# A mean over rows of 8192 floats on one core: the rows in three zones of 3, 108 and 17 per partition instead of two of 111 and 17, with another first and last load and three stores

## The chip, the core and the metric

The kernel runs on one core of a Trainium2 chip. That core has a TensorE (not used here), VectorE (DVE), ScalarE (ACT), GpSimd (POOL) and SyncE (SP), and sixteen DMA engines that move data between the memory in which the input lies and the on-chip buffers of 128 partitions. SP issues all DMAs of this kernel. The metric is the device time of one execution in microseconds, lower is better; shown are the median of several runs and one execution under the hardware profiler.

## The reference

```python
x = np.random.randn(64, 256, 8192).astype(np.float32)
def reference(x):
    return np.mean(x, axis=2)
```

The input is 16384 rows (64 x 256) of 8192 floats, 32 KiB each, 512 MiB in all. Each row becomes one number, its mean; the output has 64 KiB.

## The kernel before

**Zones.** The 16384 rows are dealt to 128 partitions, 128 rows to each. They are dealt in zones: a zone of n rows per partition covers 128 x n adjacent rows of the input, and partition p takes n adjacent rows of it, so neighbouring partitions read n x 32 KiB apart. There are two zones, of 111 and 17 rows (`ZONE`, `FROM`; `EARLY` and `LATE` are their sizes). Rows are counted per partition from 0 to 127; `rows_of(n, k)` names rows n to n + k - 1 of all partitions, which must lie in one zone.

**Buffers.** `two` holds two rows per partition (8 MiB in all), `four` holds four (16 MiB). Each is single: it is loaded anew when those who read it are done. `two_free` and `four_free` count who is done, `two_sem` and `four_sem` count landed loads (16 for each DMA). `res` takes the sum of each row, in the order of the rows; `scaled` takes the first zone's means, `ends` the second's, `fin` the last piece of the last row and its partial sums. `turn` takes three sums of a round before they are copied to `res`.

**Who sums.** DVE sums both rows of `two` with one reduction (`pair`, L169), and rows 0 to 2 of `four` with a helper, `halves` (L151), that adds the two halves of a row and sums the result in one instruction (`quad` calls it row by row). ScalarE sums the fourth row of `four` with an activation that accumulates (`row`, L218). After the loop, in `REST`, DVE takes two rows of `four` and ScalarE two. GpSimd multiplies the sums by 1/8192 (L91 for the first zone, L97 for the second).

**Order.** The order is written out by hand on SP's queue:

1. rows 111 and 110 into `two` in three DMAs of 1, 3 and 4 MiB (L109 to L111; `first_sem`), then rows 0 to 3 into `four` (L112, `second_sem`);
2. a loop of 17 rounds of six rows: wait until `two` is free, load two rows (L115, L116), wait until `four` is free, load four (L117, L118);
3. `REST`: loads of 2, 4, 2, 4 and 2 rows (112, 106, 114, 116, 120), waiting likewise (L124, L127);
4. rows 122 and 123 into the front half of `four` (`HALF`, L129), rows 124 and 125 into `two` (`LASTP`, L131);
5. the last two rows, 126 and 127, in five pieces at `cuts` (L136). The first holds row 126 and the first quarter of row 127. The later ones have 3840, 1280, 576 and 448 columns, the last of them into `fin`, the others into the back half of `four`;
6. when GpSimd has scaled the first zone and the fourth piece has landed, the store of `scaled` (L141); when `late_sem` says that `ends` is complete, the store of `ends` (L143); then the wait for both (L144).

DVE and ScalarE split each piece of the last row between them (`mine` gives ScalarE's columns); the partial sums go beside the last piece in `fin`, so that one last `halves` over 456 columns, already scaled, gives the mean of row 127 (L151, output `ends`). It waits for the last piece and for `NPART` partial sums on `last_sem`.

Of the kernel before, what the change touches and what calls it, by code (L numbers as in the profile page):

```python
# [6 lines left out]
ADD = mybir.AluOpType.add  # L7
X = mybir.AxisListType.X
# [3 lines left out]
def bass_global_avg_pool_1d_kernel(  # L12
# [4 lines left out]
    P = 128  # L17
    ALIGN = 4096
    B, C, L = x.shape
    rows = B * C  # L20
# [3 lines left out]


    OWN = rows // P
    ZONE = [111, 17]
    FROM = [0, ZONE[0]]
    EARLY, LATE = ZONE
    ROUNDS = (ZONE[0] - 9) // 6  # L30
    REST = [(112, 2), (106, 4), (114, 2), (116, 4), (120, 2)]
    HALF, LASTP = 122, 124
    assert rows % P == 0 and sum(ZONE) == OWN and 8 + 6 * ROUNDS == ZONE[0] - 1
    FIRST = L // 4


    U = L // 256
    cuts = [0, L + 64 * U, L + 184 * U, L + 224 * U, L + 242 * U, 2 * L]
    mine = [64 * U, 43 * U, 13 * U, 4 * U]
    LAST = cuts[5] - cuts[4]  # L40
    NPART = 8

    flat = x.rearrange("b c l -> (b c) l")
    out_flat = out.rearrange("b c -> (b c)")
# [4 lines left out]
    out_zone = [  # L49
        out_flat[P * f : P * (f + n)].rearrange("(p r) -> p r", p=P)  # L50
        for f, n in zip(FROM, ZONE)
    ]

    with ExitStack() as ctx:
        sb = lambda n, s: ctx.enter_context(nc.sbuf_tensor(n, s, F32))
        sem = lambda n: ctx.enter_context(nc.semaphore(n))
        res = sb("res", [P, OWN - 1])
        scaled = sb("scaled", [P, EARLY])
        ends = sb("ends", [P, LATE])
        fin = sb("fin", [P, LAST + NPART])  # L60
# [12 lines left out]
        first_sem = sem("first_sem")  # L73
        second_sem = sem("second_sem")
        chunk_sems = [sem(f"chunk_sem{c}") for c in range(4)]
# [6 lines left out]
        tail = four[:, 2 * L : 4 * L]  # L82
        part = lambda n: fin[:, LAST + n : LAST + n + 1]

        eng = nc.gpsimd
        eng.sem_inc(turn_sem, 2)
        eng.memset(part(NPART - 1), 0.0).then_inc(last_sem, 1)  # L89
        eng.wait_ge(four_free, 4)  # L90
        eng.tensor_scalar(  # L91
            scaled[:], res[:, 0:EARLY], inv, None, op0=mybir.AluOpType.mult
        ).then_inc(pool_sem, 1)
        eng.wait_ge(two_free, 5)
        eng.wait_ge(four_free, 6)
        eng.wait_ge(owned_sem, 4)
        eng.tensor_scalar(  # L97
            ends[:, 0 : LATE - 1], res[:, EARLY : OWN - 1], inv, None,
            op0=mybir.AluOpType.mult,
# [2 lines left out]

        eng = nc.sync
        def rows_of(n, k):
            z = 1 if n >= FROM[1] else 0
            return zone[z][:, (n - FROM[z]) * L : (n - FROM[z] + k) * L]

        a, z = rows_of(ZONE[0] - 1, 1), rows_of(ZONE[0], 1)
        eng.dma_start(two[:, L : L + FIRST], z[:, 0:FIRST]).then_inc(first_sem, 16)  # L109
        eng.dma_start(two[:, L + FIRST : 2 * L], z[:, FIRST:L]).then_inc(first_sem, 16)  # L110
        eng.dma_start(two[:, 0:L], a).then_inc(first_sem, 16)  # L111
        eng.dma_start(four[:], rows_of(0, 4)).then_inc(second_sem, 16)  # L112
        src = rows_of(4, 6 * ROUNDS).rearrange("p (i w) -> p i w", i=ROUNDS)
        with eng.Fori(0, ROUNDS) as i:
            eng.wait_ge(two_free, 1).then_inc(two_free, -1)  # L115
            eng.dma_start(two[:], src[:, bass.ds(i, 1), 0 : 2 * L]).then_inc(two_sem, 16)  # L116
# [12 lines left out]
        eng.dma_start(four[:, 0 : 2 * L], rows_of(HALF, 2)).then_inc(four_sem, 16)  # L129
        eng.wait_ge(two_free, 5)  # L130
        eng.dma_start(two[:], rows_of(LASTP, 2)).then_inc(two_sem, 16)  # L131
        last = rows_of(OWN - 2, 2)
        for c in range(5):
            a, z = cuts[c], cuts[c + 1]
            dst = tail[:, a:z] if c < 4 else fin[:, 0:LAST]
            eng.dma_start(dst, last[:, a:z]).then_inc(  # L136
                chunk_sems[c] if c < 4 else last_sem, 16
            )
        eng.wait_ge(pool_sem, 1)
        eng.wait_ge(chunk_sems[3], 16)  # L140
        eng.dma_start(out_zone[0], scaled[:]).then_inc(out_sem, 16)  # L141
        eng.wait_ge(late_sem, 2)
        eng.dma_start(out_zone[1], ends[:]).then_inc(out_sem, 16)  # L143
        eng.wait_ge(out_sem, 32)  # L144


        eng = nc.vector

        def halves(ap, to, done=None, scale=1.0):
            n = ap.shape[1] // 2  # L150
            made = eng.tensor_tensor_reduce(  # L151
                ap[:, 0:n],
                ap[:, 0:n],
                ap[:, n : 2 * n],
                scale=scale,
                scalar=0.0,
                op0=ADD,
                op1=ADD,
                accum_out=to,
            )  # L160
            if done is not None:
                made.then_inc(done, 1)

        rows_in = lambda ap: ap.rearrange("p (j l) -> p j l", l=L)
        at = lambda n, k: res[:, n : n + k]
        sums = res[:, 4 : 4 + 6 * ROUNDS].rearrange("p (i w) -> p i w", i=ROUNDS)

        def pair(to, ap=two[:]):
            eng.tensor_reduce(to, rows_in(ap), X, ADD).then_inc(two_free, 1)  # L169

        def quad(to, done=four_free):
            for j, ap in enumerate(to):
                halves(
                    four[:, j * L : (j + 1) * L], ap, done if j == len(to) - 1 else None
                )

        eng.wait_ge(first_sem, 48)
        pair(at(ZONE[0] - 1, 2))
        eng.wait_ge(second_sem, 16)
        quad([at(j, 1) for j in range(3)])  # L180
        with eng.Fori(0, ROUNDS) as i:
            now = sums[:, bass.ds(i, 1), :]
            eng.wait_ge(two_sem, 16).then_inc(two_sem, -16)  # L183
# [3 lines left out]
            quad([turn[:, j : j + 1] for j in range(3)], turn_sem)  # L187
            eng.wait_ge(turn_sem, 1).then_inc(four_free, 1)
            eng.tensor_copy(  # L189
                now[:, :, 2:5], turn[:].rearrange("p (i w) -> p i w", i=1)  # L190
            ).then_inc(turn_sem, 1)
        for k, (n, size) in enumerate(REST):
            eng.wait_ge(two_sem if size == 2 else four_sem, 16 * (k // 2 + 1))
            if size == 4:
                quad([at(n, 1), at(n + 1, 1)])
            elif k < len(REST) - 1:
                pair(at(n, 2))
            else:
                pair(at(n, 1), two[:, 0:L])
        eng.wait_ge(four_sem, 48)  # L200
        eng.tensor_reduce(  # L201
            at(HALF, 2), rows_in(four[:, 0 : 2 * L]), X, ADD
        ).then_inc(owned_sem, 1)
        eng.wait_ge(two_sem, 64)
        eng.tensor_reduce(at(LASTP, 1), two[:, 0:L], X, ADD).then_inc(owned_sem, 1)  # L205
        eng.wait_ge(chunk_sems[0], 16)
        halves(tail[:, 0:L], res[:, OWN - 2 : OWN - 1], owned_sem)
        for c in range(1, 4):
            eng.wait_ge(chunk_sems[c], 16)
            halves(tail[:, cuts[c] + mine[c] : cuts[c + 1]], part(3 + c), last_sem)  # L210
        eng.wait_ge(last_sem, 16 + NPART)
        halves(fin, ends[:, LATE - 1 : LATE], late_sem, inv)

# [1 line left out]
        eng = nc.scalar  # L215

        def row(ap, to):
            return eng.activation(ap, ap, COPY, accum_out=to)  # L218

        fourth, second = four[:, 3 * L : 4 * L], two[:, L : 2 * L]  # L220
        eng.wait_ge(second_sem, 16)
        row(fourth, at(3, 1)).then_inc(four_free, 1)
        with eng.Fori(0, ROUNDS) as i:
            eng.wait_ge(four_sem, 16).then_inc(four_sem, -16)  # L224
            eng.sem_inc(go_sem, 1)
            row(fourth, sums[:, bass.ds(i, 1), 5:6]).then_inc(four_free, 1)
        for k, (n, size) in enumerate(REST):
            if size == 4:
                eng.wait_ge(four_sem, 16 * (k // 2 + 1))
                row(four[:, 2 * L : 3 * L], at(n + 2, 1))  # L230
                row(fourth, at(n + 3, 1)).then_inc(four_free, 1)
        eng.wait_ge(two_sem, 48)
        row(second, at(REST[-1][0] + 1, 1)).then_inc(two_free, 1)
        eng.wait_ge(two_sem, 64)
        row(second, at(LASTP + 1, 1)).then_inc(owned_sem, 1)
        for c in range(4):
            eng.wait_ge(chunk_sems[c], 16)
            a = cuts[c] if c else L
            ap = tail[:, a : a + mine[c]]
            eng.activation(ap, ap, COPY, accum_out=part(c)).then_inc(last_sem, 1)  # L240


# [26 lines left out]
```

## Time and profile before

| | |
|---|---|
| median of three runs | 1242.95 us (1242.9 to 1242.98) |
| the profiled execution, its own time | 1243.15 us |
| its span, first to last instruction | 1241.8 us |
| moved by DMA | 536.94 MB, 432 GB/s over the span |
| busy: DVE, ACT, POOL | 643.0, 176.5, 2.3 us |

The profile is that of one execution. In its rows from the timeline the first number is the start in us from the beginning of the span, the second the duration in us; then come engine, line of the kernel, operation, output and input with their shapes (partitions x elements), and in brackets how long the engine had been idle and what ended that. "SPq" rows are DMA issues on SP: their duration is that of issuing, not of the transfer. A wait in the loop shows as "ACTq" or "DVEq", the engine's own sequencer; the data that it waited for came by DMA. In the row of the queue stand packets, megabytes and the share of the sixteen engines' span that the packets took. In the table of DMA issues, the last number is the time from issue to landing.

### The profile page before, as it was taken

The page shows a single profiled execution, that of the slowest core. Times are in us where ns is not written, and L with a number is a line of the kernel's source. Part 1 is how long each engine was busy: PE and PEld are TensorE (multiplying, and loading weights), DVE is VectorE, ACT ScalarE, POOL GpSimd, SP SyncE. Part 2 cuts the span into 40 slices and gives each one's busy share as a digit, 9 for nine tenths or more (in the row PEclk, how much of TensorE's full clock was granted, in tenths as well). Part 3 has the DMA queues.
Part 4 walks back from the last instruction along what each step waited for, and adds up shares of the span by engine and source line. Part 5 has one row for each costly group of instructions (what it writes and reads, how often), then busy time and mean ns, then how long its engine had stood idle before and what let it go on. Part 6 is the DMA issues. An engine that isn't in the chain of part 4 may idle for free. (4 is left out here: it accounts for less than half of the span.)

```text
span 1241.8 us, 713 instructions
## 1 busy us (share of the span) xinstructions
DVE 643.0 (52%) x166; ACT 176.5 (14%) x57; POOL 2.3 (0%) x7
## 2 busy tenths in 40 slices
DVE  2373836454544637383736454554638383625257
ACT  0021020202020202012020202020202102040423
POOL 0000000000000000000000000000000000000000
DMA  9999999999999999999999999999999999999998
GB/s 405 439 439 439 439 431 414 439 439 439 439 439 422 422 439 439 439 439 439 422 422 439 439 439 439 439 422 422 439 439 439 439 439 424 420 439 439 439 439 374
DMA packets 10048, 536.94 MB, mean 432 GB/s; under 512 B 1088, under 2 KB 1216, under 8 KB 1472
## 3 DMA queue, kind: packets, MB, share of 16 engines
q1 hardware_dynamic: 10048, 536.94, 99.8%
HBM read 536.87 MB, written 0.07 MB: 432 GB/s over the span
## 5 line engine op out<-in xcount | busy, mean ns | idle before, releaser
L151 DVE CUSTOM_DVE_ANT_0 four<-four 128x4096 f32<-128x4096 f32 (+3 forms) x62 | 260.5, 4248 | 434.7 <-DVEq L186 366.7
L169 DVE TENSOR_REDUCE res<-two 128x16384 f32 (+2 forms) x21 | 353.1, 16814 | 145.4 <-DVEq L183 96.3
L218 ACT ACTIVATE four<-four 128x8192 f32<-128x8192 f32 x22 | 154.6, 7029 | 1017.9 <-ACTq L224 864.3
L201 DVE TENSOR_REDUCE res<-four 128x2 f32<-128x16384 f32 x1 | 17.2, 17220 | 10.6 <-DMA four<-in_x_dram 10.6
L218 ACT ACTIVATE two<-two 128x8192 f32<-128x8192 f32 x2 | 14.1, 7030 | 36.7 <-DMA two<-in_x_dram 36.7
L205 DVE TENSOR_REDUCE res<-two 128x1 f32<-128x8192 f32 x1 | 8.7, 8686 | 2.1 <-DMA two<-in_x_dram 2.1
L240 ACT ACTIVATE four<-four 128x2048 f32<-128x2048 f32 (+3 forms) x4 | 4.1, 1030 | 7.7 <-DMA four<-in_x_dram 7.5
L189 DVE COPY res<-turn 128x3 f32 x17 | 2.9, 170 | 4.2 <-DVE turn L151 4.2
L151 DVE DVE_READ_ACCUMULATOR2_ANT turn<- 128x1 f32 x51 | 4.2, 83 | 0.0
L218 ACT ACTIVATION_READ_ACCUMULATOR four<-four (+1 forms) x22 | 4.1, 187 | 0.0
L91 POOL TENSOR_SCALAR scaled<-res 128x111 f32<-128x111 f32 x1 | 0.5, 503 | 1117.6 <-ACT four L218 1117.6
L97 POOL TENSOR_SCALAR ends<-res 128x16 f32<-128x16 f32 x1 | 1.5, 1499 | 117.9 <-DVE res L151 117.9
L218 ACT ACT_TABLE_LOAD x1 | 1.3, 1283 | 0.7 <-PEq L254 0.7
L240 ACT ACTIVATION_READ_ACCUMULATOR four<-four 128x1 f32 x4 | 0.7, 186 | 0.0
L151 DVE DVE_READ_ACCUMULATOR2_ANT res<- 128x1 f32 x8 | 0.7, 82 | 0.0
L151 DVE CUSTOM_DVE_ANT_0 fin<-fin 128x228 f32<-128x228 f32 x1 | 0.4, 397 | 0.2 <-ACT four L240 0.2
L218 ACT ACTIVATION_READ_ACCUMULATOR two<-two 128x1 f32 x2 | 0.4, 186 | 0.0
L151 DVE DVE_READ_ACCUMULATOR2_ANT fin<- 128x1 f32 x3 | 0.2, 82 | 0.0
L254 POOL MEMSET const-bfloat16-1.0<- 128x1 bf16 x1 | 0.1, 101 | 0.0
L254 POOL MEMSET const-uint8-127<- 128x1 uint8 x1 | 0.1, 101 | 0.0
L254 POOL MEMSET const-float32-0.0<- 128x1 f32 x1 | 0.1, 99 | 0.2 <-issue 0.2
L89 POOL MEMSET fin<- 128x1 f32 x1 | 0.1, 98 | 0.4 <-POOLq L254 0.4
(2 smaller groups left out, 0.2 us busy)
## 6 DMA issues: line engine op xcount, KB each, us to landing
four<-in_x_dram SPq DMA_DIRECT2D x1, 5120.0 KB, 41.6
two<-in_x_dram SPq DMA_DIRECT2D x1, 4096.0 KB, 20.9
two<-in_x_dram SPq DMA_DIRECT2D x1, 3072.0 KB, 11.7
four<-in_x_dram SPq DMA_DIRECT2D x1, 1920.0 KB, 45.7
two<-in_x_dram SPq DMA_DIRECT2D x1, 1024.0 KB, 4.9
four<-in_x_dram SPq DMA_DIRECT2D x1, 640.0 KB, 46.8
four<-in_x_dram SPq DMA_DIRECT2D x21, 44.1
two<-in_x_dram SPq DMA_DIRECT2D x21, 40.2
```

What stands on the lines that cost most here:

```text
L89: eng.memset(part(NPART - 1), 0.0).then_inc(last_sem, 1)
L91: eng.tensor_scalar(scaled[:], res[:, 0:EARLY], inv, None, op0=mybir.AluOpType.mult).then_inc(pool_sem, 1)
L97: eng.tensor_scalar(ends[:, 0 : LATE - 1], res[:, EARLY : OWN - 1], inv, None, op0=mybir.AluOpType.mult,).then_inc(late_sem, 1)
L151: made = eng.tensor_tensor_reduce(ap[:, 0:n], ap[:, 0:n], ap[:, n : 2 * n], scale=scale, scalar=0.0, op0=ADD, op1=ADD, accum_out=to,)
L169: eng.tensor_reduce(to, rows_in(ap), X, ADD).then_inc(two_free, 1)
L189: eng.tensor_copy(now[:, :, 2:5], turn[:].rearrange("p (i w) -> p i w", i=1)).then_inc(turn_sem, 1)
L201: eng.tensor_reduce(at(HALF, 2), rows_in(four[:, 0 : 2 * L]), X, ADD).then_inc(owned_sem, 1)
L205: eng.tensor_reduce(at(LASTP, 1), two[:, 0:L], X, ADD).then_inc(owned_sem, 1)
L218: return eng.activation(ap, ap, COPY, accum_out=to)
L240: eng.activation(ap, ap, COPY, accum_out=part(c)).then_inc(last_sem, 1)
L254: nc = _bacc.Bacc("TRN2", target_bir_lowering=False, num_devices=1)
```

## The change

The zones become 3, 108 and 17 rows per partition. The three rows of the first zone are loaded first, in pieces of 1, 3 and 8 MiB, into the first three rows of `four`; DVE sums rows 0 and 1 with `halves`, ScalarE row 2. Nothing is loaded into `two` ahead of the loop; GpSimd increments `two_free` once at its start, so that the loop's first load of `two` can be issued. The loop has 18 rounds, rows 3 to 110: in it partitions read 108 x 32 KiB apart. `REST` loads 2, 4, 2, 4 and 2 rows of the last zone, and `pair` sums both rows of its last load. Then rows 125 and 126 go into the front half of `four` (DVE sums the first, ScalarE the second), and row 127 alone comes in five pieces of 3072, 2816, 1280, 576 and 448 columns into the third row of `four` and `fin`. ScalarE takes 800, 416 and 128 columns of the second to fourth piece; a zero stands for its share of the first. `scaled` is stored with two DMAs, of 3 and of 108 columns, `ends` as before.

```diff
-    ZONE = [111, 17]
-    FROM = [0, ZONE[0]]
-    EARLY, LATE = ZONE
-    ROUNDS = (ZONE[0] - 9) // 6
-    REST = [(112, 2), (106, 4), (114, 2), (116, 4), (120, 2)]
-    HALF, LASTP = 122, 124
+    ZONE = [3, 108, 17]
+    HEAD, LOOPED, LATE = ZONE
+    FROM = [0, HEAD, HEAD + LOOPED]
+    EARLY = HEAD + LOOPED
+    ROUNDS = LOOPED // 6
+    REST = [(111, 2), (113, 4), (117, 2), (119, 4), (123, 2)]
+    PAIR, ONE = 125, 127
...
-    cuts = [0, L + 64 * U, L + 184 * U, L + 224 * U, L + 242 * U, 2 * L]
-    mine = [64 * U, 43 * U, 13 * U, 4 * U]
-    LAST = cuts[5] - cuts[4]
-    NPART = 8
+    cuts = [0, 3072, 5888, 7168, 7744, L]
+    mine = [0, 800, 416, 128]
+    PIECES = len(mine)
+    LAST = cuts[-1] - cuts[-2]
+    NPART = 2 * PIECES
...
+        row_at = lambda j: four[:, j * L : (j + 1) * L]
+        tail = row_at(2)
...
         eng = nc.gpsimd
+        eng.sem_inc(two_free, 1)
         eng.sem_inc(turn_sem, 2)
-        eng.memset(part(NPART - 1), 0.0).then_inc(last_sem, 1)
+        eng.memset(part(0), 0.0).then_inc(last_sem, 1)
...
-        eng.wait_ge(two_free, 5)
+        eng.wait_ge(two_free, 4)
         eng.wait_ge(four_free, 6)
-        eng.wait_ge(owned_sem, 4)
+        eng.wait_ge(owned_sem, 2)
...
-        a, z = rows_of(ZONE[0] - 1, 1), rows_of(ZONE[0], 1)
-        eng.dma_start(two[:, L : L + FIRST], z[:, 0:FIRST]).then_inc(first_sem, 16)
-        eng.dma_start(two[:, L + FIRST : 2 * L], z[:, FIRST:L]).then_inc(first_sem, 16)
-        eng.dma_start(two[:, 0:L], a).then_inc(first_sem, 16)
-        eng.dma_start(four[:], rows_of(0, 4)).then_inc(second_sem, 16)
-        src = rows_of(4, 6 * ROUNDS).rearrange("p (i w) -> p i w", i=ROUNDS)
+        head = rows_of(0, HEAD)
+        for a, z in ((0, FIRST), (FIRST, L), (L, HEAD * L)):
+            eng.dma_start(four[:, a:z], head[:, a:z]).then_inc(first_sem, 16)
+        src = rows_of(HEAD, 6 * ROUNDS).rearrange("p (i w) -> p i w", i=ROUNDS)
...
-        eng.dma_start(four[:, 0 : 2 * L], rows_of(HALF, 2)).then_inc(four_sem, 16)
-        eng.wait_ge(two_free, 5)
-        eng.dma_start(two[:], rows_of(LASTP, 2)).then_inc(two_sem, 16)
-        last = rows_of(OWN - 2, 2)
-        for c in range(5):
+        eng.dma_start(four[:, 0 : 2 * L], rows_of(PAIR, 2)).then_inc(four_sem, 16)
+        last = rows_of(ONE, 1)
+        for c in range(PIECES + 1):
...
-        eng.wait_ge(chunk_sems[3], 16)
-        eng.dma_start(out_zone[0], scaled[:]).then_inc(out_sem, 16)
+        eng.wait_ge(chunk_sems[-1], 16)
+        eng.dma_start(out_zone[0], scaled[:, 0:HEAD]).then_inc(out_sem, 16)
+        eng.dma_start(out_zone[1], scaled[:, HEAD:EARLY]).then_inc(out_sem, 16)
         eng.wait_ge(late_sem, 2)
-        eng.dma_start(out_zone[1], ends[:]).then_inc(out_sem, 16)
-        eng.wait_ge(out_sem, 32)
+        eng.dma_start(out_zone[2], ends[:]).then_inc(out_sem, 16)
+        eng.wait_ge(out_sem, 48)
...
-        sums = res[:, 4 : 4 + 6 * ROUNDS].rearrange("p (i w) -> p i w", i=ROUNDS)
+        sums = res[:, HEAD : HEAD + 6 * ROUNDS].rearrange("p (i w) -> p i w", i=ROUNDS)
...
         eng.wait_ge(first_sem, 48)
-        pair(at(ZONE[0] - 1, 2))
-        eng.wait_ge(second_sem, 16)
-        quad([at(j, 1) for j in range(3)])
+        some([at(0, 1), at(1, 1)])
...
         eng.wait_ge(four_sem, 48)
-        eng.tensor_reduce(
-            at(HALF, 2), rows_in(four[:, 0 : 2 * L]), X, ADD
-        ).then_inc(owned_sem, 1)
-        eng.wait_ge(two_sem, 64)
-        eng.tensor_reduce(at(LASTP, 1), two[:, 0:L], X, ADD).then_inc(owned_sem, 1)
-        eng.wait_ge(chunk_sems[0], 16)
-        halves(tail[:, 0:L], res[:, OWN - 2 : OWN - 1], owned_sem)
-        for c in range(1, 4):
+        some([at(PAIR, 1)], owned_sem)
+        for c in range(PIECES):
...
-        eng.wait_ge(second_sem, 16)
-        row(fourth, at(3, 1)).then_inc(four_free, 1)
+        eng.wait_ge(first_sem, 48)
+        row(row_at(2), at(2, 1)).then_inc(four_free, 1)
...
-        eng.wait_ge(two_sem, 48)
-        row(second, at(REST[-1][0] + 1, 1)).then_inc(two_free, 1)
-        eng.wait_ge(two_sem, 64)
-        row(second, at(LASTP + 1, 1)).then_inc(owned_sem, 1)
-        for c in range(4):
+        eng.wait_ge(four_sem, 48)
+        row(row_at(1), at(PAIR + 1, 1)).then_inc(owned_sem, 1)
+        for c in range(1, PIECES):
```

`some` is `quad` under another name: it calls `halves` on the first rows of `four`, one per output, and reports with the last.

More of the change, by code (lines that the diff above doesn't have):

```diff
@@ L26, in bass_global_avg_pool_1d_kernel @@
     OWN = rows // P
-    ZONE = [111, 17]
-    FROM = [0, ZONE[0]]
-    EARLY, LATE = ZONE
-    ROUNDS = (ZONE[0] - 9) // 6
-    REST = [(112, 2), (106, 4), (114, 2), (116, 4), (120, 2)]
-    HALF, LASTP = 122, 124
-    assert rows % P == 0 and sum(ZONE) == OWN and 8 + 6 * ROUNDS == ZONE[0] - 1
-    FIRST = L // 4
-    U = L // 256
-    cuts = [0, L + 64 * U, L + 184 * U, L + 224 * U, L + 242 * U, 2 * L]
-    mine = [64 * U, 43 * U, 13 * U, 4 * U]
-    LAST = cuts[5] - cuts[4]
-    NPART = 8
+    ZONE = [3, 108, 17]
[5 more added lines that the diff above has]
+    PAIR, ONE = 125, 127
+    assert rows % P == 0 and sum(ZONE) == OWN and LOOPED == 6 * ROUNDS
+    FIRST = L // 4
+    cuts = [0, 3072, 5888, 7168, 7744, L]
[3 more added lines that the diff above has]
+    NPART = 2 * PIECES
     flat = x.rearrange("b c l -> (b c) l")
@@ L73, in bass_global_avg_pool_1d_kernel @@
         first_sem = sem("first_sem")
-        second_sem = sem("second_sem")
-        chunk_sems = [sem(f"chunk_sem{c}") for c in range(4)]
+        chunk_sems = [sem(f"chunk_sem{c}") for c in range(PIECES)]
         owned_sem = sem("owned_sem")
@@ L104, in rows_of @@
         def rows_of(n, k):
-            z = 1 if n >= FROM[1] else 0
+            z = max(j for j in range(3) if n >= FROM[j])
             return zone[z][:, (n - FROM[z]) * L : (n - FROM[z] + k) * L]
-        a, z = rows_of(ZONE[0] - 1, 1), rows_of(ZONE[0], 1)
[L109 to L112, printed above, removed]
-        src = rows_of(4, 6 * ROUNDS).rearrange("p (i w) -> p i w", i=ROUNDS)
+        head = rows_of(0, HEAD)
+        for a, z in ((0, FIRST), (FIRST, L), (L, HEAD * L)):
+            eng.dma_start(four[:, a:z], head[:, a:z]).then_inc(first_sem, 16)
+        src = rows_of(HEAD, 6 * ROUNDS).rearrange("p (i w) -> p i w", i=ROUNDS)
         with eng.Fori(0, ROUNDS) as i:
@@ L128, in bass_global_avg_pool_1d_kernel @@
         eng.wait_ge(four_free, 6)
-        eng.dma_start(four[:, 0 : 2 * L], rows_of(HALF, 2)).then_inc(four_sem, 16)
-        eng.wait_ge(two_free, 5)
-        eng.dma_start(two[:], rows_of(LASTP, 2)).then_inc(two_sem, 16)
-        last = rows_of(OWN - 2, 2)
-        for c in range(5):
+        eng.dma_start(four[:, 0 : 2 * L], rows_of(PAIR, 2)).then_inc(four_sem, 16)
+        last = rows_of(ONE, 1)
+        for c in range(PIECES + 1):
             a, z = cuts[c], cuts[c + 1]
-            dst = tail[:, a:z] if c < 4 else fin[:, 0:LAST]
+            dst = tail[:, a:z] if c < PIECES else fin[:, 0:LAST]
             eng.dma_start(dst, last[:, a:z]).then_inc(
-                chunk_sems[c] if c < 4 else last_sem, 16
+                chunk_sems[c] if c < PIECES else last_sem, 16
             )
         eng.wait_ge(pool_sem, 1)
-        eng.wait_ge(chunk_sems[3], 16)
-        eng.dma_start(out_zone[0], scaled[:]).then_inc(out_sem, 16)
+        eng.wait_ge(chunk_sems[-1], 16)
+        eng.dma_start(out_zone[0], scaled[:, 0:HEAD]).then_inc(out_sem, 16)
+        eng.dma_start(out_zone[1], scaled[:, HEAD:EARLY]).then_inc(out_sem, 16)
         eng.wait_ge(late_sem, 2)
-        eng.dma_start(out_zone[1], ends[:]).then_inc(out_sem, 16)
-        eng.wait_ge(out_sem, 32)
+        eng.dma_start(out_zone[2], ends[:]).then_inc(out_sem, 16)
+        eng.wait_ge(out_sem, 48)
         eng = nc.vector
@@ L165, in bass_global_avg_pool_1d_kernel, with pair, some @@
         at = lambda n, k: res[:, n : n + k]
-        sums = res[:, 4 : 4 + 6 * ROUNDS].rearrange("p (i w) -> p i w", i=ROUNDS)
-        def pair(to, ap=two[:]):
-            eng.tensor_reduce(to, rows_in(ap), X, ADD).then_inc(two_free, 1)
-        def quad(to, done=four_free):
+        sums = res[:, HEAD : HEAD + 6 * ROUNDS].rearrange("p (i w) -> p i w", i=ROUNDS)
+        def pair(to):
+            eng.tensor_reduce(to, rows_in(two[:]), X, ADD).then_inc(two_free, 1)
+        def some(to, done=four_free):
             for j, ap in enumerate(to):
-                halves(
-                    four[:, j * L : (j + 1) * L], ap, done if j == len(to) - 1 else None
-                )
+                halves(row_at(j), ap, done if j == len(to) - 1 else None)
         eng.wait_ge(first_sem, 48)
-        pair(at(ZONE[0] - 1, 2))
-        eng.wait_ge(second_sem, 16)
-        quad([at(j, 1) for j in range(3)])
+        some([at(0, 1), at(1, 1)])
         with eng.Fori(0, ROUNDS) as i:
@@ L186, in bass_global_avg_pool_1d_kernel @@
             eng.wait_ge(turn_sem, 2).then_inc(turn_sem, -2)
-            quad([turn[:, j : j + 1] for j in range(3)], turn_sem)
+            some([turn[:, j : j + 1] for j in range(3)], turn_sem)
             eng.wait_ge(turn_sem, 1).then_inc(four_free, 1)
@@ L194, in bass_global_avg_pool_1d_kernel @@
             if size == 4:
-                quad([at(n, 1), at(n + 1, 1)])
-            elif k < len(REST) - 1:
+                some([at(n, 1), at(n + 1, 1)])
+            else:
                 pair(at(n, 2))
-            else:
-                pair(at(n, 1), two[:, 0:L])
         eng.wait_ge(four_sem, 48)
-        eng.tensor_reduce(
-            at(HALF, 2), rows_in(four[:, 0 : 2 * L]), X, ADD
-        ).then_inc(owned_sem, 1)
-        eng.wait_ge(two_sem, 64)
-        eng.tensor_reduce(at(LASTP, 1), two[:, 0:L], X, ADD).then_inc(owned_sem, 1)
-        eng.wait_ge(chunk_sems[0], 16)
-        halves(tail[:, 0:L], res[:, OWN - 2 : OWN - 1], owned_sem)
-        for c in range(1, 4):
+        some([at(PAIR, 1)], owned_sem)
+        for c in range(PIECES):
             eng.wait_ge(chunk_sems[c], 16)
-            halves(tail[:, cuts[c] + mine[c] : cuts[c + 1]], part(3 + c), last_sem)
+            halves(
+                tail[:, cuts[c] + mine[c] : cuts[c + 1]], part(PIECES + c), last_sem
+            )
         eng.wait_ge(last_sem, 16 + NPART)
@@ L218, in row @@
             return eng.activation(ap, ap, COPY, accum_out=to)
-        fourth, second = four[:, 3 * L : 4 * L], two[:, L : 2 * L]
-        eng.wait_ge(second_sem, 16)
-        row(fourth, at(3, 1)).then_inc(four_free, 1)
+        eng.wait_ge(first_sem, 48)
+        row(row_at(2), at(2, 1)).then_inc(four_free, 1)
         with eng.Fori(0, ROUNDS) as i:
@@ L225, in bass_global_avg_pool_1d_kernel @@
             eng.sem_inc(go_sem, 1)
-            row(fourth, sums[:, bass.ds(i, 1), 5:6]).then_inc(four_free, 1)
+            row(row_at(3), sums[:, bass.ds(i, 1), 5:6]).then_inc(four_free, 1)
         for k, (n, size) in enumerate(REST):
@@ L229, in bass_global_avg_pool_1d_kernel @@
                 eng.wait_ge(four_sem, 16 * (k // 2 + 1))
-                row(four[:, 2 * L : 3 * L], at(n + 2, 1))
-                row(fourth, at(n + 3, 1)).then_inc(four_free, 1)
-        eng.wait_ge(two_sem, 48)
-        row(second, at(REST[-1][0] + 1, 1)).then_inc(two_free, 1)
-        eng.wait_ge(two_sem, 64)
-        row(second, at(LASTP + 1, 1)).then_inc(owned_sem, 1)
-        for c in range(4):
+                row(row_at(2), at(n + 2, 1))
+                row(row_at(3), at(n + 3, 1)).then_inc(four_free, 1)
+        eng.wait_ge(four_sem, 48)
+        row(row_at(1), at(PAIR + 1, 1)).then_inc(owned_sem, 1)
+        for c in range(1, PIECES):
             eng.wait_ge(chunk_sems[c], 16)
-            a = cuts[c] if c else L
-            ap = tail[:, a : a + mine[c]]
+            ap = tail[:, cuts[c] : cuts[c] + mine[c]]
             eng.activation(ap, ap, COPY, accum_out=part(c)).then_inc(last_sem, 1)
```

1 line of the change is left out of this document (removed).

## The prediction

> **What bounds the kernel now.** I read the page from the top: shares of the span, the 40 slices, the queue, then the chain of waits.
>
> ```profile
> span 1241.8 us, 713 instructions
> DVE 643.0 (52%) x166; ACT 176.5 (14%) x57; POOL 2.3 (0%) x7
> DMA  9999999999999999999999999999999999999998
> q1 hardware_dynamic: 10048, 536.94, 99.8%
> DMA 14%; DVE 5%; SPq 0%; ACT 0%; issue 0%; DVEq 0%
> ```
>
> The queue's packets fill 99.8% of the sixteen DMA engines' time; DVE has work for half the span. The chain hands over from buffer to buffer ("DMA two", then "DVE res" on it, then the DMA which that freed). Its DVE steps are no stalls: while DVE reduces `two`, the transfer into `four` runs. Whether the stream ever stops is read from landings, so I went to the timeline, ScalarE's rows, since each ScalarE row on `four` starts when `four` has landed.
>
> ```profile
> 22.56 17.22 DVE L169 TENSOR_REDUCE res<-two 128x2 f32<-128x16384 f32 x1 [22.56 <-DMA two<-in_x_dram]
> 61.19 7.03 ACT L218 ACTIVATE four<-four 128x8192 f32<-128x8192 f32 x1 [59.19 <-DMA four<-in_x_dram]
> 119.38 7.03 ACT L218 ACTIVATE four<-four 128x8192 f32<-128x8192 f32 x1 [51.07 <-ACTq L224]
> 177.33 7.03 ACT L218 ACTIVATE four<-four 128x8192 f32<-128x8192 f32 x1 [50.82 <-ACTq L224]
> ...
> 1104.31 7.03 ACT L218 ACTIVATE four<-four 128x8192 f32<-128x8192 f32 x1 [50.59 <-DMA four<-in_x_dram]
> 1162.26 7.03 ACT L218 ACTIVATE four<-four 128x8192 f32<-128x8192 f32 x1 [43.81 <-DMA four<-in_x_dram]
> ...
> 1220.21 7.03 ACT L218 ACTIVATE two<-two 128x8192 f32<-128x8192 f32 x1 [31.52 <-DMA two<-in_x_dram]
> ```
>
> The reader is to see one constant rate. `four` (16 MiB: 128 partitions, four rows of 32 KiB) took 61.19 - 22.56 = 38.63 us, 2.414 us per MiB. A round of 24 MiB took 177.33 - 119.38 = 57.95 us in the loop and 1162.26 - 1104.31 = 57.95 us in the rest; 24 x 2.414 = 57.94. The input is 16384 rows of 32 KiB, 512 MiB: 512 x 2.414 = 1236.1 us. The first 8 MiB take 19.3 us and land at 22.56, so the steady stream begins, as it were, at 3.25 us. 3.25 + 1236.1 = 1239.4. The rows of the end confirm it:
>
> ```profile
> 1232.30 4.43 DVE L151 CUSTOM_DVE_ANT_0 four<-four 128x4096 f32<-128x4096 f32 x1 [3.40 <-DMA four<-in_x_dram]
> 1236.87 1.35 ACT L240 ACTIVATE four<-four 128x1376 f32<-128x1376 f32 x1 [2.56 <-DMA four<-in_x_dram]
> 1236.87 1.44 DVE L151 CUSTOM_DVE_ANT_0 four<-four 128x1232 f32<-128x1232 f32 x1
> 1236.92 1.50 POOL L97 TENSOR_SCALAR ends<-res 128x16 f32<-128x16 f32 x1 [117.90 <-DVE res L151]
> 1238.41 0.55 ACT L240 ACTIVATE four<-four 128x416 f32<-128x416 f32 x1
> 1239.14 0.31 ACT L240 ACTIVATE four<-four 128x128 f32<-128x128 f32 x1
> 1239.14 0.39 DVE L151 CUSTOM_DVE_ANT_0 four<-four 128x224 f32<-128x224 f32 x1
> 1239.19 0.35 SPq L141 DMA_DIRECT2D out_dram<-scaled  x1
> 1239.72 0.40 DVE L151 CUSTOM_DVE_ANT_0 fin<-fin 128x228 f32<-128x228 f32 x1 [0.17 <-ACT four L240]
> 1240.15 0.34 SPq L143 DMA_DIRECT2D out_dram<-ends  x1
> ```
>
> The last piece is summed from 1239.72 (0.3 above the bare sum, for the small pieces), the store is issued at 1240.15, and with 1.6 us to landing the span ends at 1241.8. So the span is 3.2 of start, 1236.5 of unbroken stream, 2.1 of end. An edit can move the time only by breaking the stream, changing its rate, or changing the 5.3 us around it.
>
> **Head.** Removed: the pair of rows 110 and 111 into `two` in three pieces, rows 0 to 3 into `four`, a DVE reduction of 17.22 us, one halving and one wait. Added: three pieces of 1, 3 and 8 MiB into `four`, and one semaphore increment on GpSimd ahead of its first memset, at which nothing waits before SP is done issuing.
>
> ```profile
> 0.73 0.39 SPq L109 DMA_DIRECT2D two<-in_x_dram  x1
> 1.17 0.42 SPq L110 DMA_DIRECT2D two<-in_x_dram  x1
> 1.65 0.42 SPq L111 DMA_DIRECT2D two<-in_x_dram  x1
> 2.11 0.59 SPq L112 DMA_DIRECT2D four<-in_x_dram  x1
> ...
> 69.89 4.42 DVE L151 CUSTOM_DVE_ANT_0 four<-four 128x4096 f32<-128x4096 f32 x1
> 74.24 0.08 DVE L151 DVE_READ_ACCUMULATOR2_ANT res<- 128x1 f32 x1
> 74.55 0.39 SPq L118 DMA_DIRECT2D four<-in_x_dram  x1
> 80.73 17.22 DVE L169 TENSOR_REDUCE res<-two 128x16384 f32 x1 [6.41 <-DVEq L183]
> ```
>
> The first two pieces have the same sizes and issue times as now. 12 MiB land at 3.25 + 12 x 2.414 = 32.2. Behind them the loop's first 8 MiB into `two` are issued at 2.1 (the fourth issue's place), or a little later for the loop's set-up, and land at 51.5. DVE halves two rows, 2 x 4.35 (69.89 to 74.24 is such a step), to 40.9 with the accumulator read at 41.0; ScalarE's row takes 7.1, to 39.3. SP issues `four` 0.23 later (74.32 to 74.55), at 41.2. That is 10.3 us before the queue would be empty. Today the same issue came at 74.55, 6.2 before the landing at 80.73, and the next `four` landed 38.65 later: no gap. Cost 0. The cover is 10.3 us; beyond it each us late is a us lost. Downward: issue ends at 1.12, the stream's effective start is 3.25, so 2.1 us; a store's whole way to landing is 1.6, so at most 0.5 could go if the first rows, now close together in memory, ramp faster. I take 0, with the other end -0.5, and +0.5 by symmetry if they ramp worse.
>
> **Loop and rest.** 18 rounds instead of 17 add 57.95 us, and everything else shrinks by as much: the whole is still 512 MiB. The number of input DMAs is equal too: now 3 + 1 + 34 + 5 + 1 + 1 + 5 = 50, then 3 + 36 + 5 + 1 + 5 = 50, so no issue or completion is added to the stream. Within a round nothing changes but the column offset of the sums in `res` and the distance between partitions in memory (below). The last pair of the rest will be reduced by DVE alone, 17.22 us instead of 8.69 beside ScalarE's 7.03 (last rows of the next fence). It delays no transfer, because `two` isn't loaded again.
>
> **End.** The last five pieces end as now: 576 and 448 columns last, 1280 before. I lay the times back from 1239.72 with 2.414 per MiB and the 0.19 us that today's five pieces cost (1239.72 - 1220.21 - 8 x 2.414). The pair of rows 125 and 126 lands at 1239.72 - 9.66 - 0.19 = 1229.9; rows 123 and 124 at 1210.6; rows 119 to 122 at 1191.2.
>
> ```profile
> 1169.28 7.01 ACT L218 ACTIVATE four<-four 128x8192 f32<-128x8192 f32 x1
> 1176.20 0.19 ACT L218 ACTIVATION_READ_ACCUMULATOR four<-four 128x1 f32 x1
> 1176.41 0.33 SPq L129 DMA_DIRECT2D four<-in_x_dram  x1
> 1181.57 7.03 ACT L218 ACTIVATE two<-two 128x8192 f32<-128x8192 f32 x1 [5.18 <-DMA two<-in_x_dram]
> 1181.58 8.69 DVE L169 TENSOR_REDUCE res<-two 128x1 f32<-128x8192 f32 x1 [10.54 <-DMA two<-in_x_dram]
> ```
>
> The pair is issued when ScalarE has done two rows on `four`, 14.15 us after its landing as here, at 1205.4, 5.2 before the queue runs dry; today's lead is 1181.57 - 1176.41 = 5.2 and the stream went on (1220.21 - 1181.57 = 38.64 for 16 MiB). The five pieces follow at once, where today they stood behind another wait. DVE is on rows 123 and 124 until 1227.8, 2.1 us before the pair lands; if that margin were gone, its summing would be late by the excess. Then the halving runs to 1234.3, and the first piece (landed 1233.5, 1536 element pairs, 1.44 + 304 x 2.99 / 2864 = 1.76 us) to 1236.1. The second lands at 1236.9 (1008 pairs, 1.2 us), before the third at 1238.4. ScalarE's row ends at 1237.0 and its 800 columns (0.55 + 384 x 0.80 / 960 = 0.87, and 0.19 for the read) at 1238.1, 0.3 before the third piece. GpSimd scales from 1237.2 to 1238.7, against a need at 1240.1. All of it lies under the pieces still in flight: cost 0.
>
> **Three stores.** `scaled` goes out as 3 and 108 columns, both behind the wait for the fourth piece, both ahead of the wait that the last store stands behind on SP.
>
> ```profile
> out_dram<-scaled SPq DMA_DIRECT2D x1, 55.5 KB, 1.6
> out_dram<-ends SPq DMA_DIRECT2D x1, 8.5 KB, 1.6
> ```
>
> The first is issued at 1239.19, the second 0.39 to 0.48 later (0.35 and the gap between the issues at 0.73, 1.17, 1.65), so SP is free at 1239.93 to 1240.02, before 1240.12, when DVE has finished. Both sizes land in 1.6. The cover is some 0.1 us. Bounds: 0, and one whole issue, +0.35; nothing is removed here that could give a gain. I take 0.05, nearer the first, as SP's gaps are short.
>
> **Row distance in memory.** In the loop, partitions were 111 rows (3552 KiB) apart and become 108 rows (3456 KiB). The trace has no such distance. The nearest rows are the two above: 3552 KiB in the loop and 544 KiB (17 rows) in the rest give the same 57.95. I take 0; the upper end is the slowest round in the trace, the first, 119.38 - 61.19 = 58.19, 0.24 above the others: 18 x 0.24 = 4.3 us. A gain is excluded as far as these rows go: six-fold different distances run at one rate.
>
> The sum on the profiled execution: span 1241.8 + 0 + 0 + 0 + 0.05 + 0 = 1241.85; that execution took 1243.15, 1.35 outside its span, and lies 0.2 above the median of 1242.95. So 1243.0.
>
> **Rivals.**
>
> 1. *The new distance slows the loop* (slower). If partitions 108 rows apart, a multiple of 128 KiB, collide where odd multiples of 32 KiB don't, each of 18 rounds is longer; at 0.24 us each the time is 1247.3. It decides from 0.14 us per round (2.5 / 18). For it: nothing here has tried the distance. Against: the two distances that were tried agree within 0.01 us, and the factor of two that is added is small.
>
> The Trainium skill has such a rule ("DMA: Bandwidth & Descriptors", Latency and other measured facts): row pitches that are large powers of two cost DMA rate, 207 GB/s at 512 KiB against 214 in full and 103 at 4 MiB; by the first of these, as an estimate, the loop would lose 3.4%, 35 us. It names powers of two, and 3456 KiB is 27 times 128 KiB, so I read it as weak here.
>
> 2. *The third store ends last.* SP is still issuing when DVE is done, or the store is late to land: +0.35, 1243.3. For it: 0.1 us of cover. Against: the issue rows of 0.35.
>
> 3. *The first bytes ramp faster* from three adjacent rows: -0.5, 1242.5. For it: the 2.1 us of start; against: same pieces, same issues.
>
> 4. *The halving or ScalarE's row is late at the end*: were the 0.3 us before the third piece overrun by as much again, 1243.3. Against: it lands ahead on today's durations.
>
> **How the numbers follow.** Forecast of no change 0.72, at 1243.0; rival 2 0.08, rival 3 0.07, rival 4 0.04, all within 0.2% (2.5 us, about what a measurement of this kernel tells from no change). Rival 1 has 0.07 and is the slower side; 0.02 stays for faster, which would need half of the 5.3 us around the stream to vanish. That gives same 0.91, slower 0.07, faster 0.02. The range goes from 1242.4 (rival 3) to 1244.2: rival 2, the +0.5 of a worse ramp and, for rival 1 in small, a tenth of its price, 0.4. It leaves out rival 1 in full and the faster cases, 0.09, and some of the edges.
>
> **What would show it.** Right: a landing of the first `four` near 32 us, `two` near 51.5, rounds of 57.95, fin's halving starting within 0.3 of 1239.7, the last store issued 0.03 after it ends. Wrong: rounds longer than 58.1 (rival 1); a halving of `four` that waits for DMA over 38.7 us after the one before (a gap in the stream); the last store issued right after the second (rival 2).

## The result and the profile after

The changed kernel takes 1245.08 us (median of 21 runs, 1244.85 to 1245.48) against 1242.92 (21 runs, 1242.87 to 1243.12): 2.16 us more, a ratio of 1.0018 with a 95% interval of 1.0011 to 1.0024. It is slower, by less than the 0.2% that the prediction took as the limit of measurement, but by over eight times the spread of the runs before. The profiled execution has a span of 1243.6 against 1241.8 (its own time is 1244.91 against 1243.15, so 1.76 more).

The stream first, in ScalarE's rows of the changed kernel's timeline (start, duration, engine, line, operation):

```profile
32.18 7.03 ACT L207 ACTIVATE four<-four 128x8192 f32<-128x8192 f32 x1 [30.17 <-DMA four<-in_x_dram]
90.44 7.03 ACT L207 ACTIVATE four<-four 128x8192 f32<-128x8192 f32 x1 [51.14 <-ACTq L212]
148.40 7.03 ACT L207 ACTIVATE four<-four 128x8192 f32<-128x8192 f32 x1 [50.84 <-ACTq L212]
...
1191.29 7.03 ACT L207 ACTIVATE four<-four 128x8192 f32<-128x8192 f32 x1 [43.80 <-DMA four<-in_x_dram]
...
1229.95 7.03 ACT L207 ACTIVATE four<-four 128x8192 f32<-128x8192 f32 x1 [24.52 <-DMA four<-in_x_dram]
```

The head lands at 32.18, a round takes 148.40 - 90.44 = 57.96, and the pair of rows 125 and 126 lands at 1229.95. The last 16 MiB ahead of that took 1229.95 - 1191.29 = 38.66. The stream is as before. Now the end, in the same timeline and below it in the changed kernel's table of DMA issues (KB, then us from issue to landing):

```profile
1239.29 0.34 SPq L139 DMA_DIRECT2D out_dram<-scaled  x1
1239.68 0.43 SPq L140 DMA_DIRECT2D out_dram<-scaled  x1
1239.79 0.40 DVE L150 CUSTOM_DVE_ANT_0 fin<-fin 128x228 f32<-128x228 f32 x1
...
1240.22 0.36 SPq L142 DMA_DIRECT2D out_dram<-ends  x1
```

```profile
out_dram<-scaled SPq DMA_DIRECT2D x1, 54.0 KB, 2.9
out_dram<-scaled SPq DMA_DIRECT2D x1, 1.5 KB, 1.9
out_dram<-ends SPq DMA_DIRECT2D x1, 8.5 KB, 3.3
```

The last halving starts 0.07 later than before (1239.79 against 1239.72), the last store is issued 0.07 later (1240.22 against 1240.15). But the last landing, after the same 8.5 KB to the same addresses, now comes 3.3 us after the issue where it came after 1.6. 0.07 + 1.7 is the whole difference of the spans. All stores count on one semaphore, `out_sem`, so the table's landings are the times of its 16th, 32nd and 48th increment, dealt out in the order of issue: the last one is sure, but which of the stores it was that came late the table can't tell. SP's waits say it too, the row of the changed kernel above, that of the kernel before below:

```profile
SPq L143 <- DMA out_dram<-ends: 3.0, 1, 3.0
```

```profile
SPq L144 <- DMA out_dram<-ends: 1.3, 1, 1.3
```

So the question was which property of the three stores makes them late. The theory: the 12-byte pieces. Partition p stores three floats right behind those of partition p - 1, so 128 pieces from all sixteen DMA engines fall into 1.5 KB; such writes queue up, and the stores behind them on each engine wait ("dense theory"). Against it: three stores are one too many, whatever they hold (count); 12 bytes are too small, wherever they go (size); the 432-byte pieces at their new addresses are slow (wide); or the difference lies in the head, the loop or the last row, and the late landing is chance (start).

### The profile page after: what moved, and what is told of

It reads as the page before. It is cut to its first block, busy times and chain, and to the rows that moved or that the text cites. A ratio compares the mean times of both kernels' runs of the same rounds, so it can differ in the third digit from the quotient of the medians.

```text
span 1243.6 us, 742 instructions
## 1 busy us (share of the span) xinstructions
DVE 636.0 (51%) x171; ACT 173.9 (14%) x55; POOL 1.8 (0%) x7
## 5 line engine op out<-in xcount | busy, mean ns | idle before, releaser
L150 DVE CUSTOM_DVE_ANT_0 four<-four 128x4096 f32<-128x4096 f32 (+2 forms) x65 | 270.7, 4211 | 466.7 <-DVEq L181 388.2
L168 DVE TENSOR_REDUCE res<-two 128x16384 f32 (+1 forms) x21 | 361.6, 17221 | 133.0 <-DVEq L178 106.4
L207 ACT ACTIVATE four<-four 128x8192 f32<-128x8192 f32 x24 | 168.7, 7029 | 1064.3 <-ACTq L212 915.2
```

Of the source, the lines that this page charges most:

```text
L150: made = eng.tensor_tensor_reduce(ap[:, 0:n], ap[:, 0:n], ap[:, n : 2 * n], scale=scale, scalar=0.0, op0=ADD, op1=ADD, accum_out=to,)
L168: eng.tensor_reduce(to, rows_in(two[:]), X, ADD).then_inc(two_free, 1)
```

## The experiments

All times are medians; the kernels were timed beside the kernel before, which took 1242.91 (experiments 1 to 4), 1242.96 (5 to 8) and 1242.97 us (9 to 12). Differences are to that.

**1. The 12-byte store out of the end.** It goes ahead of the load of rows 125 and 126, so that it runs behind the load of rows 123 and 124.

```diff
+        eng.wait_ge(pool_sem, 1)
+        eng.dma_start(out_zone[0], scaled[:, 0:HEAD]).then_inc(out_sem, 16)
         eng.wait_ge(four_free, 6)
         eng.dma_start(four[:, 0 : 2 * L], rows_of(PAIR, 2)).then_inc(four_sem, 16)
...
-        eng.wait_ge(pool_sem, 1)
         eng.wait_ge(chunk_sems[-1], 16)
-        eng.dma_start(out_zone[0], scaled[:, 0:HEAD]).then_inc(out_sem, 16)
```

> The store of the three head columns (128 adjacent pieces of 12 bytes, 1.5 KB in all) is moved ahead of the load of rows 125 and 126, so that it runs some 30 us before the end; the other two stores stay. Dense theory (many tiny adjacent pieces queue up in memory and hold back the stores behind them): the last store lands in 1.6 to 1.8 us again instead of 3.3, time 1243.0 to 1243.4. Count theory (three stores close together are one too many, whatever their size): two are left at the end as before the change, so also 1243.0 to 1243.4; this run alone does not part the two. Wide theory (the 432-byte pieces at their new addresses are slow): still 1244.7 to 1245.2. Start theory (the difference lies ahead of the stores, in the stream): still 1244.7 to 1245.2.

Measured: 1244.24 (+1.33), which fits none of the numbers. The profile parts two things. The table of DMA issues of this kernel:

```profile
out_dram<-scaled SPq DMA_DIRECT2D x1, 54.0 KB, 1.6
out_dram<-scaled SPq DMA_DIRECT2D x1, 1.5 KB, 41.8
out_dram<-ends SPq DMA_DIRECT2D x1, 8.5 KB, 1.4
```

Both stores left at the end land in 1.6 and 1.4: the wide theory falls, and the landing is cured by taking the 12-byte store away (its own 41.8 is the queue ahead of it). But the stream became late, in ScalarE's rows and in the last halving:

```profile
1191.24 7.03 ACT L207 ACTIVATE four<-four 128x8192 f32<-128x8192 f32 x1 [43.77 <-DMA four<-in_x_dram]
...
1230.95 7.03 ACT L207 ACTIVATE four<-four 128x8192 f32<-128x8192 f32 x1 [25.58 <-DMA four<-in_x_dram]
...
1240.80 0.40 DVE L150 CUSTOM_DVE_ANT_0 fin<-fin 128x228 f32<-128x228 f32 x1 [0.16 <-ACT four L225]
```

1230.95 - 1191.24 = 39.71, 1.05 more than the 38.66 above: 1.5 KB held the loads up for a microsecond. In its new place the store still has a price.

**2. The 432-byte store out of the end**, by the same edit with the other store.

> The mirror image: the store of the 108 columns goes ahead of the load of rows 125 and 126, the 12-byte store stays at the end with the last one. Dense theory: the last store is still held back, landing 2.8 to 3.3 us after its issue, time 1244.5 to 1245.1. Count theory: two stores at the end, 1243.0 to 1243.4. Wide theory: 1243.0 to 1243.4.

Measured: 1243.82 (+0.91), between the theories' numbers. The 12-byte store landed in 2.3, the last in 1.9 (1.4 to 1.6 without it). The count theory's 1243.0 to 1243.4 doesn't hold, and the dense store alone costs less than with the wide one behind it. Part of the 0.91 is the stream: this execution had a last halving at 1240.27.

**3. Three wide stores.** The kernel before, its first store split.

```diff
-        eng.dma_start(out_zone[0], scaled[:]).then_inc(out_sem, 16)
+        eng.dma_start(out_zone[0][:, 0:55], scaled[:, 0:55]).then_inc(out_sem, 16)
+        eng.dma_start(out_zone[0][:, 55:EARLY], scaled[:, 55:EARLY]).then_inc(out_sem, 16)
...
-        eng.wait_ge(out_sem, 32)
+        eng.wait_ge(out_sem, 48)
```

> The kernel before, its first store split into two of 55 and 56 columns (220 and 224 bytes per partition), so that three stores stand at the end with the issue times of the changed kernel, none of tiny pieces. Dense theory and size theory (any 12-byte piece is slow): 1242.9 to 1243.2, last landing 1.6 to 1.8 us. Count theory: 1244.5 to 1245.2, last landing about 3.3 us.

Measured: 1242.94 (+0.03). The count theory is out: a third store costs nothing at this place.

**4. The same 12-byte pieces, 444 bytes apart.** As 3, with the cut at 3 instead of 55.

> The kernel before, its first store split into 3 and 108 columns: the same 12-byte pieces, but 444 bytes apart in memory instead of adjacent. Dense theory: 1242.9 to 1243.3, last landing 1.6 to 1.9 us. Size theory: 1244.5 to 1245.2, last landing about 3.3 us. Count theory: likewise 1244.5 to 1245.2.

Measured: 1242.95 (+0.04). The size theory is out as well. Rows of this kernel, its two first stores as in the changed one, to the byte, but for the distance between the pieces:

```profile
out_dram<-scaled SPq DMA_DIRECT2D x1, 54.0 KB, 1.7
out_dram<-scaled SPq DMA_DIRECT2D x1, 1.5 KB, 1.4
out_dram<-ends SPq DMA_DIRECT2D x1, 8.5 KB, 1.5
```

**5. Two zones, all else as changed.** Head of three rows, 18 rounds, last pair and last row stay; the first two zones are one of 111 again, stored at once.

```diff
-    ZONE = [3, 108, 17]
+    ZONE = [EARLY, LATE]
...
-        eng.dma_start(out_zone[0], scaled[:, 0:HEAD]).then_inc(out_sem, 16)
-        eng.dma_start(out_zone[1], scaled[:, HEAD:EARLY]).then_inc(out_sem, 16)
+        eng.dma_start(out_zone[0], scaled[:]).then_inc(out_sem, 16)
...
-        eng.wait_ge(out_sem, 48)
+        eng.wait_ge(out_sem, 32)
```

> The changed kernel with its first two zones made one of 111 rows again: same head of three rows, same 18 rounds, same last pair and row, but rows 111 apart in memory while reading and two stores at the end, 444 and 68 bytes per partition. Dense theory: the whole loss is the dense store's, so 1242.8 to 1243.1, last landing 1.6. Theory that the new head, loop or last row also costs: above 1243.3.

Measured: 1243.04 (+0.08; 1242.93 to 1243.16). Head, rounds and end of the change cost nothing that can be told; all but 0.08 of the 2.16 goes with the third zone. The last store landed in 1.4.

**6. The dense store second**, behind the wide one.

> The changed kernel with the two first stores in the other order: 108 columns, then the dense 12-byte pieces, then the last. Dense theory: the 432-byte pieces now land in 1.6, the dense ones in 2.0 to 2.5, the last in 1.9 to 3; time 1243.4 to 1244.5, below 1245.08, since fewer bytes stand behind the dense store. Sum theory (the delay is that of all three together, whatever their order): 1244.8 to 1245.3.

Measured: 1244.43 (+1.47), as the dense theory has it, and not the sum theory. The wide store landed in 1.7, the dense one in 1.9, the last in 2.5 (against 2.9, 1.9 and 3.3 in the changed kernel's order).

**7 and 8. The dense store with only the last one behind it, and the same pieces 64 bytes apart.** Run 7 drops the store of 108 columns; run 8 puts in its and the dense store's place:

```diff
-        eng.dma_start(out_zone[0], scaled[:, 0:HEAD]).then_inc(out_sem, 16)
-        eng.dma_start(out_zone[1], scaled[:, HEAD:EARLY]).then_inc(out_sem, 16)
+        apart = out_flat[0 : 16 * P].rearrange("(p r) -> p r", p=P)
+        eng.dma_start(apart[:, 0:HEAD], scaled[:, 0:HEAD]).then_inc(out_sem, 16)
...
-        eng.wait_ge(out_sem, 48)
+        eng.wait_ge(out_sem, 32)
```

> The changed kernel without its store of 108 columns, so that the means of rows 3 to 110 are left out of the output: the dense 12-byte store and the last one alone. Dense theory: the dense store lands in 2 to 2.5, the last in about 1.9; time 1243.2 to 1243.6, which is the price of the dense store with little behind it. Sum theory: 1242.9 to 1243.1.

> As the run without the store of 108 columns, but the 12-byte pieces are written 64 bytes apart (8 KB instead of 1.5 KB), which puts them elsewhere than the reference has them. Dense theory: the first store lands in 1.4 to 1.7 and the last in 1.4 to 1.7; time 1242.9 to 1243.1, below its twin with adjacent pieces by 0.3 to 0.5. Size theory, should it hold after all: as the twin.

Measured: 1243.80 (+0.84) and 1243.22 (+0.26). First and last store landed in 1.9 and 1.9 when adjacent, in 1.4 and 1.6 when 64 bytes apart. The rows of run 7, and below them those of run 8:

```profile
out_dram<-scaled SPq DMA_DIRECT2D x1, 1.5 KB, 1.9
out_dram<-ends SPq DMA_DIRECT2D x1, 8.5 KB, 1.9
```

```profile
out_dram<-scaled SPq DMA_DIRECT2D x1, 1.5 KB, 1.4
out_dram<-ends SPq DMA_DIRECT2D x1, 8.5 KB, 1.6
```

Both times are a little above what was written down, by a part that the next run looks at.

**9. The change without its dense store.** Of the three stores only the first is dropped.

> The changed kernel without its 12-byte store, so that the means of rows 0 to 2 are left out of the output: partitions still read 108 rows apart in the loop, two stores at the end. Dense theory alone: as with two zones, 1242.9 to 1243.1, last landing 1.4 to 1.6. If reading 108 rows apart also costs (some profiled executions had one to three of the first eight rounds 0.1 to 0.3 longer, none of those 111 apart): 1243.15 to 1243.4, and more scatter between runs.

Measured: 1243.26 (+0.29; 1242.9 to 1243.5), the second of the two: 1.87 of the 2.16 go with the dense store. Most of the rest shows in an early round. ScalarE's rows of this kernel (its profiled execution, 1243.5, was the slowest of the eleven):

```profile
148.53 7.03 ACT L206 ACTIVATE four<-four 128x8192 f32<-128x8192 f32 x1 [50.85 <-ACTq L211]
206.48 7.03 ACT L206 ACTIVATE four<-four 128x8192 f32<-128x8192 f32 x1 [50.83 <-ACTq L211]
264.75 7.03 ACT L206 ACTIVATE four<-four 128x8192 f32<-128x8192 f32 x1 [51.15 <-ACTq L211]
322.75 7.03 ACT L206 ACTIVATE four<-four 128x8192 f32<-128x8192 f32 x1 [50.88 <-ACTq L211]
```

One round of 264.75 - 206.48 = 58.27 among rounds of 57.95 to 58.00. The last halving came at 1240.27, half a microsecond after that of the two zones (1239.78).

**10 to 12. How dense.** As run 8, but the 12-byte pieces 32 bytes apart (run 10), sixteen columns 64 bytes apart, that is adjacent pieces of 64 bytes (run 11), one column 4 bytes apart, that is adjacent pieces of 4 bytes (run 12). The edits are run 8's with other numbers, for run 12:

```diff
+        apart = out_flat[0 : 1 * P].rearrange("(p r) -> p r", p=P)
+        eng.dma_start(apart[:, 0:1], scaled[:, 0:1]).then_inc(out_sem, 16)
```

> As the run with pieces 64 bytes apart, but 32 bytes apart (4 KB; again elsewhere than the reference has them, and the means of rows 3 to 110 left out). If two pieces in 64 bytes are enough to queue up: last landing 1.7 to 2.0 and 1243.4 to 1243.7. If it takes a denser row: 1.4 to 1.6 and 1243.1 to 1243.3, like its twin.

> Adjacent pieces again, but of 64 bytes (16 columns, 8 KB), starting at a multiple of 64; elsewhere than the reference has them, the other means of the first 111 rows left out. Dense theory (it is several pieces in one small stretch that costs, not that they touch): last landing 1.4 to 1.6, 1243.0 to 1243.3. If adjacency as such costs: last landing 1.9, 1243.6 to 1243.9.

> Denser still: one column, 128 adjacent pieces of 4 bytes, 512 bytes in all; elsewhere than the reference has them for all but partition 0, the other means of the first 111 rows left out. Dense theory: at least as long as with 12-byte pieces, first store 1.9 to 3 to landing, last 1.9 to 3, time 1243.7 to 1245. If bytes count rather than pieces in a stretch: less than with 12 bytes, 1243.2 to 1243.5.

Measured: 1243.24 (+0.27), 1243.20 (+0.23) and 1249.13 (+6.16). First and last store landed in 1.4 and 1.4 in both of the first, and in run 12, by its table of DMA issues, in

```profile
out_dram<-scaled SPq DMA_DIRECT2D x1, 0.5 KB, 6.1
out_dram<-ends SPq DMA_DIRECT2D x1, 8.5 KB, 7.4
```

Half a kilobyte in 128 pieces of 4 bytes is by far the dearest store of all: more than the 1243.7 to 1245 written down allowed for. Side by side, 128 pieces each time (4 bytes: run 12; 12 bytes: runs 7, 10 and 8; 64 bytes: run 11):

| bytes of a piece | bytes from piece to piece | lands in us | last store lands in us | time against before |
|---|---|---|---|---|
| 4 | 4 | 6.1 | 7.4 | +6.16 |
| 12 | 12 | 1.9 | 1.9 | +0.84 |
| 12 | 32 | 1.4 | 1.4 | +0.27 |
| 12 | 64 | 1.4 | 1.6 | +0.26 |
| 64 | 64 | 1.4 | 1.4 | +0.23 |

With 128 pieces each time, it is not the number of bytes (the fewest cost most) and not that the pieces touch (those of 64 bytes do): what goes with the price is how many pieces share a short stretch of memory. From 12 to 32 bytes the price is gone; between these nothing was tried, nor whether it matters that several DMA engines write into the same stretch. All five kernels read 108 rows apart, so some 0.2 to 0.3 of the last column isn't the store's (run 9).

## Why the prediction was wrong

**The stream: right.** The first four rows of the loop were issued at 41.2 and the head landed at 32.2, as worked out; the rounds, the pair at 1229.9, the halvings behind it and ScalarE's 800 columns came within 0.2 us of the times laid back from the end. Run 5 confirms it: the same head, loop and end with two zones stay within 0.08 us of the kernel before. That the stream decides and that the edits to it cancel out was the right reading.

**Three stores: the step that failed.** The prediction wrote "Both sizes land in 1.6" and bounded the new store by 0 and one issue, +0.35. The issue part held: the second store's issue ended at 1240.11, before the last halving was read out at 1240.19, and the last store was issued 0.03 after that. But 1.6 was the landing of pieces of 444 and 68 bytes, and it was carried over to pieces of 12 bytes at a distance of 12. The bound left out that a store whose kind no row showed could make the last landing late: 3.3 us instead of 1.6, so +1.7 in the profile, and 1.87 in the median, by run 9. Measured from the forecast of 1243.0, that is nearly the whole miss of 2.08.

**Rival 2 named the place and missed the price.** "The store is late to land" was among its conditions, at +0.35. What runs 3 and 4 add: neither the third store nor its small pieces would have done it; the distance between them does. The bound should have looked at both measures of the store, the piece and the step.

**Rival 1 seems to have happened, at a twentieth of its price.** Reading 108 rows apart goes with some 0.2 us, not 4.3: the four timed kernels that read so with a harmless store or none (runs 8 to 11) lie 0.23 to 0.29 above the kernel before, the one that reads 111 apart 0.08. In six of the ten profiled executions with 108, one to three rounds were 58.05 to 58.27 long, nearly all in the first 350 us; in the four with 111 all rounds after the first were at most 57.99. The load packets show it as well: of those of 64 KiB, which took 2.418 us as a rule, 47 to 97 took over 2.45 between 65 and 1200 us in these six, all in the first 400 us; in the other four with 108 it was 0 to 11, in those with 111 none or one. Why they lengthen, and why only early, isn't settled, and with the scatter of these runs (0.5 to 0.6 us) the 0.2 is a reading of several medians, not one tested difference.

**The rule on row pitches** that was weighed beside rival 1 (the Trainium skill, "DMA: Bandwidth & Descriptors", Latency and other measured facts) was rightly read as weak: by its figure for 512 KiB the loop would have lost 35 us, as an estimate, while the changed kernel's rounds after the first took 57.92 to 58.00 us, against 57.95 to 57.96 before.

**Taken as unmeasurable, 2.5 us was too coarse.** The 21 runs of the kernel before spread over 0.25 us. 2.16 us lie within the prediction's 0.2%, but they are a real loss, and the upper end of its range, 1244.2, rested on the failed bound.

**Open.** Why the 432-byte store makes the dense one dearer: alone with the last store it costs 0.84 - 0.27 = 0.57, with the wide one behind it 1.87, with the wide one ahead 1.47 - 0.27 = 1.20. That the stores behind it have to wait doesn't explain the last of these, since there too only the last store stands behind it. There the dense store was issued 0.39 later than in run 7 (1240.04 against 1239.65) and the last one at the same time (1240.57 and 1240.56), which may be a part of it.

Where the wait is not, the traces show. The DMA engines were done with all packets long before the last landing. In these rows stand the stretch of time, its length, the busy times of DVE, ACT and POOL, the clock, the DMA engines' busy share and their GB/s; they are of the kernel before, the changed kernel and run 12, each up to its end:

```profile
1241.25:1241.80 0.55, 0.00 (x0) 0.00 (x0) 0.00 (x0) 1.00 0.00 0
```

```profile
1241.35:1243.57 2.22, 0.00 (x0) 0.00 (x0) 0.00 (x0) 1.00 0.00 0
```

```profile
1241.30:1247.60 6.30, 0.00 (x0) 0.00 (x0) 0.00 (x0) 1.00 0.00 0
```

So the part of the theory that had the later stores wait on the engines isn't borne out: in the changed kernel the last store's packets start 0.86 us after its issue (1241.08), before the change 0.84 (1240.99). What comes late is the count of the landed: the first 16 increments of `out_sem` are spread over 0.17 us in run 8, 0.67 in run 7 and 2.8 in run 12. What holds them back wasn't seen.

## What to carry to other kernels

When a result is cut into zones, look at the store of each zone by its piece and its step: a zone of few rows per partition makes small adjacent pieces. Here 128 of 12 bytes cost 0.6 to 1.9 us at an end where nothing hides them, and 128 of 4 bytes some 6. Give such values to a neighbouring zone, so that the pieces lie in longer rows, as run 5 does within 0.08 us of the kernel before. And a term that no row of the trace shows is not bounded by rows of another kind: 1.6 us for 444 and for 68 bytes said nothing of 12.

## What the runs showed of the hardware

A small store in mid-stream isn't free either: 1.5 KB in adjacent 12-byte pieces behind a load of 8 MiB held the loads up by 1.05 us (run 1), while the 54 KB of 432-byte pieces at the same place cost about 0.16. ScalarE's rows of run 2, to be read like those of run 1:

```profile
1191.59 7.03 ACT L207 ACTIVATE four<-four 128x8192 f32<-128x8192 f32 x1 [43.77 <-DMA four<-in_x_dram]
...
1230.41 7.03 ACT L207 ACTIVATE four<-four 128x8192 f32<-128x8192 f32 x1 [24.68 <-DMA four<-in_x_dram]
```

1230.41 - 1191.59 = 38.82, against 38.66 with no store there. Thirty-six times the bytes cost a sixth of the time. Each of the two is one profiled execution, but run 1's median says the same: its 1.33 less run 9's 0.29 is 1.04. The delay also stands in run 1's packets: those of 64 KiB took 2.418 us each in the 10 us before the store, and up to 3.67 in the 4 us from 1210 on, while the store's own 12-byte packets, at 1209.9 to 1210.3, took 9 ns each.
